# Merge of three attention patterns: one weight store and two weight loads per merge, products on GpSimd, z_b's product in the last stage

## Chip, cores and metric

One core of one Trainium2 chip. The metric is device time of one execution in microseconds (us), the median of the runs.

## What is computed

A hybrid encoder layer over 2048 tokens of width 1024, all in float32. The normalised input is projected to the inputs of a state-space branch, to queries, keys and values, to two gates z_a and z_b and to two mixing gates. The attention branch runs three dilated window patterns for 8 slots of 64 channels and merges them by their log-sum-exps:

```python
outs, lses = [], []
for p_idx, (window, dilation) in enumerate(ATTN_PATTERNS):
    o, lse = dilated_band_attention(q[:, :, p_idx], k, v, window, dilation)
    outs.append(o)
    lses.append(lse)
wts = jax.nn.softmax(jnp.stack(lses, axis=0), axis=0)
attn = jnp.einsum('gblh,gblhd->blhd', wts, jnp.stack(outs, axis=0)).reshape(bsz, L, ATTN_WIDTH)
y_b = (attn * jax.nn.silu(z_b)) @ w_proj_attn[layer].astype(jnp.float32)
...
mix = jax.nn.sigmoid(g_a) * y_a + jax.nn.sigmoid(g_b) * y_b
x = x + (mix @ w_out[layer].astype(jnp.float32)).astype(x.dtype)
```

## The kernel before, in words

Products on TensorE (PE) are made in three passes: each factor is split into a rounded high part and a low part (`hi`, `lo`; ScalarE copies, VectorE subtracts), and `mm3` adds hi*hi, hi*lo and lo*hi. Everything between stages goes through DRAM scratch tensors.

There are three stages. The first (to about 1085 us) makes the projections and the state-space branch. The second is attention, `phase_b`: 4 pairs of heads (`hp`), for each the patterns 1, 0 and 2, for each pattern 4 blocks of 512 tokens (`quad`). A step scores (`attn_scores`; VectorE's masked minimum in line 1003, ScalarE's exponential in line 1007), transposes the probabilities on PE and copies them out of PSUM, alternately on ScalarE and VectorE (`attn_turn`, lines 1030 and 1032), and multiplies by the values (`attn_values`). Between steps PE gets filler (`run`): gate projections, then the state-space branch's GLU, then the first parts of its output projection (`ssm_part`, weights `ws`). Queries (line 960) and values (lines 965, 972) are loaded by GpSimd's (POOL's) queue, almost all else by SyncE's (SP's).

When pattern 2 of a block of a pair is done, its merge starts: 16 merges, `attn_merge(hp, r, ...)`. A merge has three parts. The first transposes the block's minima and sums, stores them in ST and loads those of all three patterns (`s6`). The second works out the three weights per token on VectorE and ScalarE (lines 1096 to 1104), stores them in AL by two transfers (line 1108), one per head, and loads them back spread over the 64 channels of each head: six transfers of 128 KB (line 1111) into three tiles `ab[2]`, `ab[1]`, `ab[0]`, which share four buffers; then it loads z_b's block. The third multiplies and adds, five operations on POOL and one on VectorE, and stores the result in ACTB:

```python
G.tensor_mul(ab[2], ab[2], o2)
G.tensor_mul(ab[1], ab[1], self.O[1][:, c])
G.tensor_add(ab[2], ab[2], ab[1])
V.tensor_mul(ab[0], ab[0], self.O[0][:, c])
G.tensor_add(ab[2], ab[2], ab[0])
G.tensor_mul(ab[2], ab[2], zb)
```

The last stage, `phase_c`, goes over 8 blocks of 256 tokens. Two blocks need one merge of each of the four pairs. `cut` loads a block of ACTB and splits it (lines 1349, 1350, the tiles `pair`), PE projects it with `wa` (matmuls that read `wah` and `wal`), VectorE mixes it with the state-space part `cm` under the gates (lines 1401 to 1404, tiles `mh`, `ml`), PE multiplies by `wo`, and VectorE adds the input `xres`.

The source order is not the order of execution: the Tile framework's scheduler (`schedule_with_timeline_sim=True`, line 1495) lists each engine's instructions anew, with the source order as priority, and puts tiles of closed pools' memory to new use. Each engine and each queue then takes its list in order, so whoever waits holds all that is listed behind it.

## Time and profile before

| what | value |
|---|---|
| runs | 2077.11 us median of 3 (2076.78 to 2082.68) |
| profiled execution | 2084.98 us, span of its instructions 2083.2 us |
| busy share of the span | PE 95%, VectorE (DVE) 62%, ScalarE (ACT) 35%, POOL 40% |
| mean granted clock of TensorE | 0.974 |
| instructions | 37578 |

The profile is of one execution. Busy time is what an engine spent inside instructions; a waiting engine is idle, and "waits" name who ended the idle time. The windows cut the span into stretches: 1200 to 1680 is most of attention, with all but the last four of its merges (first merge's products at 1225.8 us), 1680 to 1760 its end with the last four merges and the start of the last stage, 1760 to 2083 the rest of the last stage. PEclk is the granted clock, 1.00 for 2.4 GHz. The chain of waits follows back from the last instruction.

### The profile page before, as it was taken

The page shows a single profiled execution, that of the slowest core. Times are in us where ns is not written, and L with a number is a line of the kernel's source. Part 1 is how long each engine was busy: PE and PEld are TensorE (multiplying, and loading weights), DVE is VectorE, ACT ScalarE, POOL GpSimd, SP SyncE. Part 2 cuts the span into 40 slices and gives each one's busy share as a digit, 9 for nine tenths or more (in the row PEclk, how much of TensorE's full clock was granted, in tenths as well). Part 3 has the DMA queues.
Part 4 walks back from the last instruction along what each step waited for, and adds up shares of the span by engine and source line. Part 5 has one row for each costly group of instructions (what it writes and reads, how often), then busy time and mean ns, then how long its engine had stood idle before and what let it go on. Part 6 is the DMA issues. An engine that isn't in the chain of part 4 may idle for free.

```text
span 2083.2 us, 37578 instructions
## 1 busy us (share of the span) xinstructions
PE 1975.6 (95%) x13612; PEld 1764.6 (85%) x13612; DVE 1292.2 (62%) x3312; ACT 725.7 (35%) x1829; POOL 826.8 (40%) x1088
## 2 busy tenths in 40 slices
PE   6899999999999999899989999998998978999999
PEld 6788899998788889899977877876887978899997
DVE  8867575978566778587755455455567655433432
ACT  4221343333232343233326544554655632100110
POOL 4310464538636654475442346346345222000000
PEclk9999999999999999999999999999998998999999
DMA  5632464445533444634474465566676547433332
GB/s 192 195 100 73 126 198 147 121 120 158 166 109 114 153 144 141 178 114 133 130 230 138 154 180 165 166 178 179 208 204 179 161 134 233 147 114 115 117 111 76
DMA packets 272059, 312.54 MB, mean 150 GB/s; under 512 B 86594, under 2 KB 182226, under 8 KB 271874
## 3 DMA queue, kind: packets, MB, share of 16 engines
q1 hardware_dynamic: 250914, 260.39, 41.8%
q0 software_dynamic: 20960, 49.76, 8.1%
q8 instruction: 107, 1.75, 0.3%
q14 instruction: 78, 0.64, 0.1%
HBM read 202.12 MB, written 105.71 MB: 148 GB/s over the span
## 4 chain that ended last, share of the span: by engine, by line
PE 59%; DVE 16%; DMA 13%; SPq 4%; issue 3%; POOL 3%; ACT 2%; DVEq 0%; ACTq 0%; POOLq 0%
PE acc L53 39%; PE po L53 12%; PE s L53 3%; PE pp L56 3%; DMA raw<-in_w_in 2%; DVE wlo L311 2%; DMA ab<-AL 2%; SPq L513 1%; DVE zs L843 1%; DMA AL<-e 1%; DMA ACTA<-fth 1%; DVE zs L841 1%; DMA s<-ST 1%; PE y L53 1%; SPq L1111 1%
## 5 line engine op out<-in xcount | busy, mean ns | idle before, releaser
L53 PE MATMUL acc<-xh,whi 128*128 128x512 f32 (+1 forms) x960 | 376.7, 393 | 17.8 <-DVE xsc L379 8.3
L53 PE MATMUL acc<-whi,xh 128*128 128x256 f32 x1280 | 368.2, 288 | 2.9 <-ACT qr L451 2.1
L53 PE MATMUL acc<-xl,whi 128*128 128x512 f32 (+1 forms) x960 | 367.9, 384 | 1.1 <-DVE xl L208 1.1
L53 PE MATMUL acc<-xh,wlo 128*128 128x512 f32 (+1 forms) x960 | 367.3, 384 | 0.0
L53 PE MATMUL acc<-whi,xl 128*128 128x256 f32 x1280 | 364.7, 285 | 1.9 <-POOL xl L263 1.6
L53 PE MATMUL acc<-wlo,xh 128*128 128x256 f32 x1280 | 364.7, 285 | 0.0
L53 PEld LDWEIGHTS acc<-whi,xh 128*128 128x128 f32 x1280 | 247.9, 194 | 5.6 <-ACT qr L451 2.4
L53 PEld LDWEIGHTS acc<-whi,xl 128*128 128x128 f32 x1280 | 247.9, 194 | 2.5 <-POOL xl L263 1.9
L53 PEld LDWEIGHTS acc<-wlo,xh 128*128 128x128 f32 x1280 | 248.1, 194 | 0.0
L53 PEld LDWEIGHTS acc<-xh,whi 128*128 128x128 f32 x960 | 184.9, 193 | 54.0 <-issue 10.9
L1007 ACT ACTIVATE p<-p,st 128x256 f32<-128x256 f32 (+2 forms) x384 | 172.8, 452 | 143.6 <-DVE st L1003 143.2
L311 DVE TENSOR_TENSOR wlo<-raw,whi 128x512 fp32r<-128x512 f32 x168 | 151.2, 918 | 110.9 <-ACT whi L310 110.1
L53 PEld LDWEIGHTS acc<-xh,wlo 128*128 128x128 f32 x960 | 184.9, 193 | 33.7 <-issue 0.5
L53 PEld LDWEIGHTS acc<-xl,whi 128*128 128x128 f32 x960 | 185.4, 193 | 29.4 <-DVE xl L208 1.6
L310 ACT ACTIVATE whi<-raw 128x512 fp32r<-128x512 f32 x176 | 102.9, 625 | 165.7 <-DMA raw<-in_w_in 140.1
L1003 DVE CUSTOM_DVE_ANT_0 p<-s,m 128x256 f32<-128x256 f32 (+2 forms) x376 | 115.8, 358 | 68.3 <-PE s L53 45.0
L972 POOL DMA_DIRECT2D v<-V x150 | 91.7, 618 | 121.2 <-PE po L53 115.0
L53 PE MATMUL s<-kh,q 128*128 128x256 f32 (+2 forms) x400 | 104.3, 299 | 12.1 <-DVE st L1003 7.2
L53 PE MATMUL acc<-pair,wsh 128*128 128x256 f32 x512 | 99.3, 295 | 16.3 <-DVE cm L1373 11.4
L53 PE MATMUL po<-t,v 128*64 128x128 f32 (+1 forms) x1280 | 110.3, 293 | 1.8 <-ACT t L1030 0.9
L56 PE MATMUL pp<-c_ident,p 128*128 128x128 f32 (+1 forms) x640 | 94.1, 281 | 13.5 <-DVE t L1032 12.4
L53 PEld LDWEIGHTS po<-t,v 128*64 128x64 f32 (+1 forms) x1280 | 75.3, 141 | 37.2 <-issue 23.7
(331 smaller groups left out, 4392.1 us busy)
## 6 DMA issues: line engine op xcount, KB each, us to landing
raw<-in_w_in SPq DMA_DIRECT2D x176, 256.0 KB
q<-QT POOLq DMA_DIRECT2D x92, 256.0 KB, 4.2
ab<-AL SPq DMA_DIRECT2D x96, 128.0 KB
ug<-U SPq DMA_DIRECT2D x128, 64.0 KB
GA<-th SPq DMA_DIRECT2D x32, 256.0 KB
GB<-th SPq DMA_DIRECT2D x32, 256.0 KB
raw<-GB SPq DMA_DIRECT2D x32, 256.0 KB
xres<-in_x SPq DMA_DIRECT2D x32, 256.0 KB
```

Of the source, the lines that this page charges most:

```text
L53: return self.nc.tensor.matmul(*a, **k)
L56: return self.nc.tensor.transpose(*a)
L310: self.nc.scalar.activation(hi, t, AF.Copy)
L311: (eng or self.nc.vector).tensor_sub(lo, t, f(hi))
L513: nc.sync.dma_start(at(dst, d, e), f(t[64 * h:64 * h + 64]))
L841: V.tensor_tensor_scan(zs[:64, n, 2:258], r[:64].to_broadcast([64, 256]), z[:64, n], 0.0, op0=OP.mult, op1=OP.add)
L843: V.tensor_tensor_scan(zs[64:, n, 0:256][:, ::-1], r[64:].to_broadcast([64, 256]), z[64:, n, ::-1], 0.0, op0=OP.mult, op1=OP.add)
L972: (nc.gpsimd if late else nc.sync).dma_start(v[:(16 if p == 0 else 4) * (j1 - j0), m - m0], at(self.V, (base + 4 * j0) * C + c0, rows + [[ ...
L1003: self.marks["dve"] = nc.vector.tensor_tensor_reduce(pt, sc, mk, op0=OP.add, op1=OP.min, scale=-0.125, scalar=least if o else 3e38, accum_ ...
L1007: self.marks["act"] = nc.scalar.activation(pt, pt, AF.Exp, bias=st[:, 0, h, c:c + 1], scale=-1.0, accum_out=st[:, 1, h, c:c + 1])
L1111: nc.sync.dma_start(t[64 * h:64 * h + 64], at(self.AL, hp * 6 * R + p * 2 * R + h * R + 512 * r, [[0, 64], [1, 512]]))
```

## The change

AL is laid out by pair, block, pattern, head and token, so that a merge's weights lie together. A merge stores them by one transfer and loads them by two, one per head with all three patterns, into one tile `ab` with two buffers of three patterns each. All its products are on POOL, and the one with z_b is gone from it. `cut` gets a further argument: in the last stage the block of z_b is loaded whole, and POOL multiplies it with the block of ACTB ahead of the split. The tiles `zb` and `xres` are in a pool of the last stage, no longer in attention's.

```diff
--- before.py
+++ after.py
@@ -109,7 +109,7 @@
         self.KT = scr("KT", [8, 2, 2, 64, 2048])
         self.V = scr("V", [2048, 512])
         self.ST = scr("ST", [4, 3, 2, 2, 2048])
-        self.AL = scr("AL", [4, 3, 2, 2048])
+        self.AL = scr("AL", [4, 4, 3, 2, 512])
         self.ACTA = scr("ACTA", [8, 128, 4, 256])
         self.ACTB = scr("ACTB", [4, 4, 128, 512])
 
@@ -1102,24 +1102,20 @@
             V.tensor_add(mn, mn, t[:, 2])
             V.reciprocal(mn, mn)
             V.tensor_mul(e, e, vw(mn, 0, [[0, 3], [1, 8]]))
-        ab = {p: mg.tile([128, 512], F32, name="ab", bufs=4) for p in (2, 1, 0)}
+        ab = mg.tile([128, 3, 512], F32, name="ab", bufs=2)
+        o = (4 * hp + r) * 3072
+        nc.sync.dma_start(at(self.AL, o, [[8, 128], [1024, 3], [1, 8]]), e)
         for h in range(2):
-            o = hp * 6 * R + h * R + 512 * r
-            nc.sync.dma_start(at(self.AL, o, [[8, 64], [2 * R, 3], [1, 8]]), e[64 * h:64 * h + 64])
-        for p, t in ab.items():
-            for h in range(2):
-                nc.sync.dma_start(t[64 * h:64 * h + 64], at(self.AL, hp * 6 * R + p * 2 * R + h * R + 512 * r, [[0, 64], [1, 512]]))
-        zb = self.op.tile([128, 512], F32, name="zb", tag="zb", bufs=2)
-        nc.sync.dma_start(zb, self.ZB[r, hp])
+            nc.sync.dma_start(ab[64 * h:64 * h + 64], at(self.AL, o + 512 * h, [[0, 64], [1024, 3], [1, 512]]))
         yield
         c = slice(512 * r, 512 * r + 512)
+        ab = [ab[:, p] for p in range(3)]
         with self.behind():
             G.tensor_mul(ab[2], ab[2], o2)
             G.tensor_mul(ab[1], ab[1], self.O[1][:, c])
             G.tensor_add(ab[2], ab[2], ab[1])
-            V.tensor_mul(ab[0], ab[0], self.O[0][:, c])
+            G.tensor_mul(ab[0], ab[0], self.O[0][:, c])
             G.tensor_add(ab[2], ab[2], ab[0])
-            G.tensor_mul(ab[2], ab[2], zb)
         nc.sync.dma_start(self.ACTB[r, hp], ab[2])
         yield
 
@@ -1340,14 +1336,18 @@
             for _ in self.ssm_part(b, self.early[b]):
                 yield 0.32 if _ is None else 0.0
 
-    def cut(self, src, scale):
+    def cut(self, src, scale, by=None):
         nc, V = self.nc, self.nc.vector
         hi, lo = self.pair()
         nc.sync.dma_start(f(lo), src)
+        x = f(lo)
+        if by is not None:
+            x = by
+            nc.gpsimd.tensor_mul(x, x, f(lo))
         for q in range(2):
             s = slice(2 * q, 2 * q + 2)
-            nc.scalar.activation(hi[:, s], f(lo[:, s]), AF.Copy, scale=scale)
-            V.scalar_tensor_tensor(lo[:, s], f(lo[:, s]), scale, f(hi[:, s]), op0=OP.mult, op1=OP.subtract)
+            nc.scalar.activation(hi[:, s], x[:, s], AF.Copy, scale=scale)
+            V.scalar_tensor_tensor(lo[:, s], x[:, s], scale, f(hi[:, s]), op0=OP.mult, op1=OP.subtract)
         return hi, lo
 
     def proj(self, b, w, y, g, gate):
@@ -1389,7 +1389,10 @@
             wcut = lambda: self.wcut(ws[0], None, 2)
             for b in range(8):
                 nb, o = b // 2, 256 * (b % 2)
-                bb = self.cut(at(self.ACTB, nb * 4 * 128 * 512 + o, [[512, 128], [128 * 512, 4], [1, 256]]), 0.5)
+                zb = cr.tile([128, 4, 256], F32, name="zb", bufs=2)
+                io = nb * 4 * 128 * 512 + o, [[512, 128], [128 * 512, 4], [1, 256]]
+                nc.sync.dma_start(zb, at(self.ZB, *io))
+                bb = self.cut(at(self.ACTB, *io), 0.5, zb)
                 mx = self.mixes.pop(b)
                 mh = self.op.tile([128, 8, 256], F32R, name="mh", tag="o0")
                 ml = self.op.tile([128, 8, 256], F32R, name="ml", tag="o1")
@@ -1412,7 +1415,7 @@
                     s = 4 * (2 * (b % 2) + t) + nb
                     for n in range(2):
                         rows = [[NS * D, 128], [1, 512]]
-                        xr = self.op.tile([128, 512], F32, name="xres", tag="zb", bufs=2)
+                        xr = cr.tile([128, 512], F32, name="xres", bufs=2)
                         nc.sync.dma_start(xr, at(self.ins["x"], s * D + 512 * n, rows))
                         ps = po.tile([128, 512], F32, name="po")
                         for k in range(8):
```

How the instructions stand in the built programs, at three places. In these rows x2 or x6 counts equal instructions in a row, numbers behind names tell buffers apart, and lines of the changed kernel are its own (products: L1114 to L1118, the weights' store L1107 and loads L1109, z_b's load L1394 and product L1346).

VectorE at the first merge, between the minima of scores and the copies of transposed probabilities, before:

```order
L1003 ISA p_14367,st<-s,m_12503 128x192
L1003 ISA st 128x1
L1120 TENSOR_TENSOR ab<-ab,o_12518 128x512
L1096 TENSOR_TENSOR mn<-s_14246 128x8
L393 TENSOR_SCALAR th<-th 128x512
L1097 TENSOR_TENSOR mn<-mn,s_14246 128x8
L1098 TENSOR_TENSOR e<-mn,s_14246 128x24
L311 TENSOR_TENSOR wlo<-raw,whi 128x512
L1032 COPY t_14392<-pp 128x384
```

and now:

```order
L1003 ISA p_14348,st<-s,m_12503 128x192
L1003 ISA st 128x1
L1096 TENSOR_TENSOR mn<-s_14237 128x8
L1097 TENSOR_TENSOR mn<-mn,s_14237 128x8
L1098 TENSOR_TENSOR e<-mn,s_14237 128x24
L393 TENSOR_SCALAR th<-th 128x512
L311 TENSOR_TENSOR wlo<-raw,whi 128x512
L1032 COPY t_14373<-pp 128x384
```

The product of line 1120, which reads a loaded `ab`, is gone from ahead of the copy `t`.

SP at the first merges, before:

```order
L1086 DMA ST<-sr_14243 4x4x128
L1108 DMA AL<-e 64x3x8 x2
L1089 DMA s_14246<-ST 64x6x8
L1111 DMA ab<-AL 64x512 x6
L1089 DMA s_14246<-ST 64x6x8
L1086 DMA ST<-sr_14358 4x4x128
L302 DMA raw<-in_w_in 128x512 x2
L1089 DMA s_14361<-ST 64x6x8 x2
L395 DMA GA<-th 128x512
L302 DMA raw<-in_w_in 128x512
L1108 DMA AL<-e 64x3x8 x2
L1111 DMA ab<-AL 64x512 x2
```

and now:

```order
L1086 DMA ST<-sr_14234 4x4x128
L1107 DMA AL<-e 128x3x8
L1089 DMA s_14237<-ST 64x6x8
L1109 DMA ab<-AL 64x3x512 x2
L1089 DMA s_14237<-ST 64x6x8
L302 DMA raw<-in_w_in 128x512 x2
L1086 DMA ST<-sr_14339 4x4x128
L1089 DMA s_14342<-ST 64x6x8 x2
L395 DMA GA<-th 128x512
L302 DMA raw<-in_w_in 128x512
L1107 DMA AL<-e 128x3x8
L1109 DMA ab<-AL 64x3x512 x2
```

Each merge has three issues where it had eight; what lies between them is nearly as it was.

SP at the end of attention, from the last merge's weights to the last stage, before:

```order
L1346 DMA pair<-ACTB 128x4x256
L1360 DMA raw<-GB 128x2x256
L1360 DMA cg<-GA 128x2x256
L1360 DMA raw<-GB 128x2x256 x2
L1360 DMA cg<-GA 128x2x256
L1123 DMA ACTB<-ab 128x512
L1108 DMA AL<-e 64x3x8 x2
L1416 DMA xres<-in_x 128x512
L1111 DMA ab<-AL 64x512 x6
L302 DMA raw<-in_w_out 128x512 x3
L1346 DMA pair<-ACTA 128x1024
L1360 DMA raw<-GB 128x2x256
L302 DMA raw<-in_w_out 128x512 x2
L1123 DMA ACTB<-ab 128x512
```

and now:

```order
L1107 DMA AL<-e 128x3x8
L1360 DMA raw<-GB 128x2x256
L302 DMA raw<-in_w_out 128x512
L1360 DMA cg<-GA 128x2x256
L1109 DMA ab<-AL 64x3x512 x2
L1342 DMA pair<-ACTA 128x1024
L1119 DMA ACTB<-ab 128x512
L302 DMA raw<-in_w_out 128x512
L1119 DMA ACTB<-ab 128x512
L1394 DMA zb<-ZB 128x4x256
L1419 DMA xres<-in_x 128x512 x2
L1394 DMA zb<-ZB 128x4x256
```

Before, the first block of ACTB (`pair<-ACTB`) is loaded ahead of the last merge's weights, and nothing else is needed for its split. Now z_b's first load stands behind the store of the last merge (the load of the block itself still stands ahead), and on POOL the block's product stands behind the last merge's five operations.

## Rows read from the trace of the kernel before

**Rows 1.** The page, part 1: busy time, share, instructions of each engine.

```profile
PE 1975.6 (95%) x13612; PEld 1764.6 (85%) x13612; DVE 1292.2 (62%) x3312; ACT 725.7 (35%) x1829; POOL 826.8 (40%) x1088
```

**Rows 2.** Windows: length, busy PE, PEld, DVE, ACT, POOL; PE clock, DMA share, GB/s.

```profile
1200.00:1440.00 240.00, 223.80 (x1520) 177.13 (x1518) 125.56 (x484) 113.91 (x402) 120.08 (x166) 0.96 0.61 173
...
1680.00:1760.00 80.00, 61.05 (x452) 57.75 (x451) 44.45 (x93) 20.20 (x49) 27.27 (x21) 0.87 0.63 178
1760.00:2083.00 323.00, 319.45 (x1984) 288.56 (x1983) 119.61 (x177) 38.11 (x64) 0.00 (x0) 1.00 0.39 120
```

**Rows 3.** Waits of PE, 1200 to 1440: total us, times, longest.

```profile
PE pp L56 <- DVE t L1032: 14.5, 6, 3.4
```

**Rows 4.** Waits of PE, 1440 to 1680.

```profile
PE pp L56 <- DVE t L1032: 4.0, 3, 2.0
```

**Rows 5.** Waits of DVE, 1200 to 1760.

```profile
DVE ab L1120 <- DMA ab<-AL: 44.0, 11, 6.2
```

**Rows 6.** Timeline of DVE: start, us, instruction, idle before it and releaser.

```profile
1230.20 1.68 DVE L1120 TENSOR_TENSOR ab<-ab,o 128x512 f32<-128x512 f32 x1 [4.84 <-DMA ab<-AL]
...
1423.83 2.50 DVE L1120 TENSOR_TENSOR ab<-ab,o 128x512 f32<-128x512 f32 x1 [5.19 <-DMA ab<-AL]
```

**Rows 7.** Timeline of PE, after those two.

```profile
1234.86 0.38 PE L56 MATMUL pp<-c_ident,st 128*16 128x128 f32 x1 [3.35 <-DVE t L1032]
...
1426.58 1.70 PE L56 MATMUL pp<-c_ident,p 128*64 128x128 f32 x7 [3.10 <-DVE t L1032]
```

**Rows 8.** A window behind the first of these gaps.

```profile
1232.00:1242.00 10.00, 7.14 (x32) 4.85 (x33) 6.92 (x30) 3.99 (x14) 1.46 (x2) 0.66 0.41 112
```

**Rows 9.** The tile ab: ns min/median/max, first and last start; its waits.

```profile
L1117 POOL TENSOR_TENSOR ab<-ab,o x16: 1267/1284/1377, 1225.8 to 1745.1; 128x512 f32<-128x512 f32 x16
...
L1120 DVE TENSOR_TENSOR ab<-ab,o x16: 679/1188/3230, 1230.2 to 1749.4; 128x512 f32<-128x512 f32 x16
...
  DMA ab<-AL: 116.2, 29
```

**Rows 10.** Timeline of SP, 1678 to 1756: issues of the last merges' transfers.

```profile
1678.18 0.63 SPq L1086 DMA_DIRECT2D ST<-sr  x1
...
1702.32 0.46 SPq L1123 DMA_DIRECT2D ACTB<-ab  x1
...
1729.58 0.38 SPq L1346 DMA_DIRECT2D pair<-ACTB  x1
...
1736.68 1.26 SPq L1108 DMA_DIRECT2D AL<-e  x2
...
1741.16 3.67 SPq L1111 DMA_DIRECT2D ab<-AL  x6
...
1755.62 0.38 SPq L1123 DMA_DIRECT2D ACTB<-ab  x1
```

**Rows 11.** Waits of PE, 1680 to 1760.

```profile
PE acc L53 <- DVE cm L1373: 11.4, 3, 5.1
PE acc L53 <- DVE mn L1096: 4.5, 1, 4.5
PE acc L53 <- DVE raw L1401: 2.6, 1, 2.6
```

**Rows 12.** Timeline of ACT and PE: the last stage's first block.

```profile
1736.40 1.15 ACT L1349 ACTIVATE pair<-pair 128x512 fp32r<-128x512 f32 x2 [0.82 <-DMA pair<-ACTB]
...
1739.37 0.40 PE L53 MATMUL acc<-pair,wah 128*128 128x256 f32 x2
```

**Rows 13.** Timeline of SP, and the chain of waits: a later block.

```profile
1801.21 0.36 SPq L1346 DMA_DIRECT2D pair<-ACTB  x1
...
1833.38 8.63 PE acc L53 x72
```

**Rows 14.** Timeline of DVE: line 1120 in the first and last of four merges.

```profile
1695.45 1.31 DVE L1120 TENSOR_TENSOR ab<-ab,o 128x512 f32<-128x512 f32 x1 [4.53 <-DMA ab<-AL]
...
1749.44 0.69 DVE L1120 TENSOR_TENSOR ab<-ab,o 128x512 f32<-128x512 f32 x1 [5.57 <-DMA ab<-AL]
```

## The prediction

> **What bounds the kernel now.** I read the engines' busy shares first, then stages in windows, then what TensorE (PE) waited for. PE is busy 95% of the span [rows 1], so an edit that adds no PE work can only win back time in which PE stands, or runs at the lower clock. The windows say where that is: in the attention stage PE stands 16.2 us of 240 between 1200 and 1440, in the change to the last stage 19.0 us of 80, in the last stage 3.6 us of 323; the granted clock goes with it, 0.96, 0.87 and 1.00 [rows 2]. So the merges can be worth some tens of microseconds and no more.
>
> Between 1200 and 1440 nearly all of PE's standing, 14.5 us in 6 times, is a transpose waiting for DVE's copies of transposed probabilities (line 1032) [rows 3]; from 1440 to 1680 that wait is 4.0 us [rows 4]. Why is DVE late? Its largest wait in the whole attention stage is line 1120, the merge's product with pattern 0, for the loads of the weights: 44.0 us, 11 times [rows 5]. DVE takes its instructions in order, so the copies stand behind that product. The first case: DVE stood 4.84 us and started line 1120 at 1230.20; PE, which had run out of copies, stood 3.35 us until 1234.86. The last of five such pairs in this window: DVE stood 5.19 us to 1423.83, PE 3.10 us to 1426.58 [rows 6, 7]. The five take 14.0 of the 14.5 us. Behind such a gap PE also comes back slower: the granted clock was 0.66 over the 10 us from 1232, a mix of its two levels, 1.2 and 2.4 GHz [rows 8].
>
> **The change, part by part.**
>
> *The DVE product goes to POOL.* DVE then waits for no weight loads. In 1200 to 1440 that gives back the five gaps, **14.0 us**, and the clock behind them: 0.04 of 240 us is 9.6 us if every drop there is of this cause [rows 2]; nothing if other gaps keep the clock down. I take **5**, half, since other short gaps stay. In 1440 to 1680 one of three gaps, the longest with 2.0 us, follows such a wait [rows 4]: **2.0**. DVE is also relieved of 16 products of 1.19 us (median) [rows 9], 19 us in all; it is busy 126 of 240 us there [rows 2], so I count that at nothing.
>
> *POOL.* Per merge it had five operations and keeps five: one product comes from DVE, the one with z_b leaves. Each lasts about 1.28 us [rows 9], so POOL's load is unchanged. What is queued behind POOL's wait are the issues of q and v loads. That wait can grow: POOL's first product needed two of six loads, now it needs both large ones. Below, nothing is gained; above, POOL's and DVE's waits of today, 116.2 us in 29 times [rows 9], all stand on POOL and some loads of q come late. I take zero, because the weights arrive together sooner (next item), and keep the loss as a rival.
>
> *SP's queue.* Per merge two stores and six loads took 1.26 and 3.67 us of issue [rows 10], and the z_b load, taken like the one-piece store of the same size, about 0.4: some 5.3 us. Now there are one store and two loads. The nearest rows are these same loads, 0.6 each; larger ones cannot be shown here, so 1.9 to 4.9 us. I take 1.9, as the time went per issue. That is 3.4 us per merge, 54 us of queue; it is worth something only where a chain through SP ends last, at the end of the attention.
>
> *The last four merges, and z_b.* Today the store of merge 13 is issued at 1702.32, that of merge 16 at 1755.62: 17.8 us apart each [rows 10]. Take off 3.4 of SP issue and 3.4 of DVE's wait per merge (it stood 4.53 us before the first and 5.57 before the last of these four products [rows 14]; I take less, since not all four wait), and the spacing is 11 us: the last store at about 1702 + 33 = 1735. That is sooner. But the built order puts the load of z_b for the first block of the last stage behind that last store on SP, and its product behind the last merge on POOL. Today the first block needs merge 13 alone: its load goes out at 1729.58, ScalarE cuts it at 1736.40 and PE takes up the block (wah) at 1739.37 [rows 10, 12]. Now, from 1735: 0.4 issue, 5 landing (6.8 for the row just named, with its queueing), 2.6 product (twice the 512-wide 1.28) and 1.2 cut, so about 1744: **5 us later** than today, and a spell of the lower clock behind the stand, **+3.4** (6.8 us at half rate, as the 0.66 over 10 us amounts to). One later wait of today, 2.6 us for DVE's mixing of that block [rows 11], falls in the shadow: **-2.6**. PE's earlier stands in this window, 4.5 and 11.4 us [rows 11], don't count separately: they only decide how long PE waits at the block. Behind that split, on ScalarE and DVE, stand the splits of w_out's pieces, which the first output product needs; they are next to be late, but PE has 96 matmuls of the block (11 us, at the 8.63 us for 72 of [rows 13]) to cover them. Net **+6**. Bounds: a merge alone takes 24.1 us from its first store to its last (1678.18 to 1702.32), which would put the last store at 1726 and the block at 1735, -7 in all; with the last store where it is today, the block starts near 1765, +26.
>
> *The other seven blocks.* Their loads go out some 32 us before use (1801.21, used at 1833.38) [rows 13]. One more load in parallel and a 2.6 us product fit under that. Nothing counted; if the cover went, 8 times 2.6, 21 us, would be the price.
>
> Against this item speaks one row: line 1120 lasts 0.68 us at best and 3.23 at worst [rows 9], that is, DVE's two-input operations get slower when POOL works beside them. The Trainium skill, page "SBUF — State Buffer", section "Who interferes with whom", says why it may: a DVE instruction with two SBUF inputs and a GpSimd one that reads SBUF share a read port, and whichever starts second is blocked until the first is through. By that rule the eight new products could each hold a DVE instruction for their whole length, and the sum would lose up to 21 us instead of nothing; the trace agrees that such stretching happens, not that PE feels it.
>
> **Sum.** -14.0 -5 -2 +6 = -15 us. The profiled execution took 2084.98 us (span 2083.2), 7.9 above the median; the same -15 from the median 2077.11 gives **2062 us**.
>
> **Rivals.**
> - *The new wait decides (slower).* The last store does not move forward, since the last four merges still go through SP one behind another. Then z_b, loaded behind it, starts the block near 1765: +26; the gaps are won (14 and 2), the clock is not: 2077 + 26 - 16 = 2087. For it: SP also carries the gate and weight loads, in which it stands for DVE. Against it: DVE's 4 to 5 us stands are gone from the chain. Even with the clock won (21 us in all) gain turns into loss once the last store comes after about 1750 of today's time. Chance 0.16.
> - *The wait moves to POOL.* Its products stand for weights, q and v loads come late, and PE waits for scores where it now waits for copies: the 14, 5 and 2 are lost, the tail is as forecast: 2077 + 6 = 2083. For it: POOL already stands in 18 of those 29 waits. Against it: PE's 16.2 us of standing from 1200 to 1440 hold 14.5 for the copies [rows 2, 3], so a late q costs nearly nothing today. Chance 0.14.
> - *The tail shortens as well.* A last store at 1726 and the whole clock: -14 -9.6 -2 -7, so 2045. Chance 0.13.
> - *The read port holds DVE in the last stage.* Each of eight products stops a DVE operation for all of its 2.6 us and PE waits for it: 2062 + 21 = 2083. Against it: DVE is busy 120 of 323 us there [rows 2], and the output products have four accumulators to run ahead in. Chance 0.05.
> - *It does not do what it says*: the order written anew puts other waits on DVE and nothing remains but noise, 2077. Chance 0.04.
>
> **How the numbers follow.** The forecast itself has 0.48. A measurement of this kernel tells about 0.3%, 6.2 us, from no change. Faster by more: 0.44 of the forecast's 0.48, 0.13 of the short tail and 0.04 of the POOL case, which may be partial: 0.61. Slower by more: 0.13 of the new wait, 0.03 each of POOL and port: 0.19. The rest, 0.20, is within. For 8 in 10 the range runs from 2048, short of the best case, to 2086, short of the worst.
>
> **What would show it.** Right: no DVE wait for ab left; PE's waits for line 1032 from 1200 to 1440 down from 14.5 to under 3 us; clock near 1 there; the load of z_b issued after the last store, and one long stand of PE (10 to 20 us) before the first wah. Wrong: PE waiting for q or scores behind POOL; a stand above 30 us before wah, which would mean that the last merges did not get faster; or gaps in the last stage.

## The result and the profile after

The changed kernel takes 2092.8 us, the kernel before 2077.0: **ratio 1.0068, 95% interval 1.0050 to 1.0086, slower by 0.7%.** The forecast was 2062 us, range 2048 to 2086; the time lies outside it and on the other side of no change.

The profiled execution took 2090.18 us, its span is 2088.2. That is only 5.2 us more than the profiled execution of the kernel before (2084.98), though the medians differ by 15.8. That execution of before was a long one, as a second profile of it shows below, and this one is the shortest of the changed kernel's four.

The page of the changed kernel, part 1 (beside [rows 1]):

```profile
PE 1968.8 (94%) x13612; PEld 1761.1 (84%) x13612; DVE 1288.5 (62%) x3296; ACT 726.0 (35%) x1829; POOL 849.1 (41%) x1096
```

Its windows (beside [rows 2]; columns as there):

```profile
1200.00:1440.00 240.00, 226.84 (x1546) 180.73 (x1545) 120.56 (x475) 113.56 (x396) 124.61 (x168) 0.97 0.60 168
1440.00:1680.00 240.00, 224.04 (x1882) 202.65 (x1881) 162.24 (x547) 144.00 (x460) 95.14 (x133) 0.96 0.60 174
1680.00:1760.00 80.00, 47.53 (x339) 45.78 (x339) 40.13 (x70) 18.22 (x34) 29.45 (x21) 0.79 0.68 198
1760.00:2088.00 328.00, 324.45 (x2018) 293.55 (x2016) 120.65 (x176) 35.63 (x59) 16.93 (x7) 1.00 0.40 123
```

The last stage runs as before. In 1680 to 1760 PE now stands 32.5 us where it stood 19.0, and the clock is 0.79 where it was 0.87. In 1200 to 1440 it still stands 13.2 us, and the clock is 0.97. The waits of PE in that window (beside [rows 3]):

```profile
PE pp L56 <- DVE t L1032: 6.9, 3, 3.1
PE pp L56 <- DVE sr L1085: 5.6, 4, 3.2
```

The first was to fall from 14.5 to under 3 us. The second, for the copies of the transposed statistics (line 1085), was 1.1 us in the kernel before.

The waits of DVE, 1200 to 1760 (us in total, times, longest), where [rows 5] had 44.0 us for ab:

```profile
DVE p L1003 <- PE s L53: 49.7, 33, 4.2
DVE mn L1096 <- DMA s<-ST: 35.9, 8, 6.6
```

No wait for ab is left, as forecast. But line 1096, the merge's first minimum, waits 35.9 us for the loads of its statistics. In the kernel before, the same view has 16.4 us for it. In DVE's list it stands in front of the same copies as line 1120 did. One case, timeline of DVE and then of PE:

```profile
1244.13 0.27 DVE L1096 TENSOR_TENSOR mn<-s 128x8 f32<-128x8 f32 x1 [4.95 <-DMA s<-ST]
...
1249.70 0.54 DVE L1032 COPY t<-pp 128x384 f32<-128x384 f32 x1
```

```profile
1250.30 0.66 PE L56 MATMUL pp<-c_ident,p 128*128 128x128 f32 x4 [2.95 <-DVE t L1032]
```

DVE stood 4.95 us for the statistics, its copies came late, and PE stood 2.95 us for them: the picture of [rows 6, 7] with another load in it.

The longest stand of PE for a copy, later in attention, has no load behind it. Timelines of DVE and PE, and the durations of line 1153 (ns: least, median, most):

```profile
1580.64 5.50 DVE L1153 SCALAR_TENSOR_TENSOR pair<-ft,pair 128x512 fp32r<-128x512 f32 x1
```

```profile
1586.66 0.69 PE L56 MATMUL pp<-c_ident,p 128*128 128x128 f32 x2 [5.69 <-DVE t L1032]
```

```profile
L1153 DVE SCALAR_TENSOR_TENSOR pair<-ft,pair x16: 671/691/5501, 1449.1 to 1658.6; 128x512 fp32r<-128x512 f32 x16
```

This DVE operation lasted 5.50 us while POOL made merge products beside it (from 1581.19); in the second profile of this kernel (after_again, below) the longest of line 1153 is 2.12 us.

The end of attention. The tile view gives the number of an instruction, its durations, and its first and last start. First the last products of attention (they read t), then those with wah, for the kernel before:

```profile
L53 PE MATMUL po<-t,v x1280: 269/273/476, 1095.6 to 1693.0; 128*64 128x128 f32 x161, 64*64 64x128 f32 x22
...
L53 PE MATMUL acc<-pair,wah x512: 277/283/387, 1739.4 to 2058.4; 128*128 128x256 f32 x171
```

and for the changed kernel:

```profile
L53 PE MATMUL po<-t,v x1280: 269/273/476, 1093.5 to 1684.9; 128*64 128x128 f32 x161, 64*64 64x128 f32 x22
...
L53 PE MATMUL acc<-pair,wah x512: 277/283/582, 1744.9 to 2063.4; 128*128 128x256 f32 x171
```

From the last attention product to the first wah it was 46.4 us and is 60.0. I call this stretch the tail. Timelines of SP, POOL, ACT and PE in it:

```profile
1696.52 0.38 SPq L1119 DMA_DIRECT2D ACTB<-ab  x1
...
1714.43 0.36 SPq L1107 DMA_DIRECT2D AL<-e  x1
...
1721.97 1.24 SPq L1109 DMA_DIRECT2D ab<-AL  x2
...
1735.69 0.32 SPq L1119 DMA_DIRECT2D ACTB<-ab  x1
1737.93 0.37 SPq L1394 DMA_DIRECT2D zb<-ZB  x1
```

```profile
1741.84 2.34 POOL L1346 TENSOR_TENSOR zb<-zb,pair 128x1024 f32<-128x1024 f32 x1 [6.17 <-DMA zb<-ZB]
```

```profile
1744.21 1.15 ACT L1349 ACTIVATE pair<-zb 128x512 fp32r<-128x512 f32 x2 [4.37 <-POOL zb L1346]
```

```profile
1744.90 1.31 PE L53 MATMUL acc<-pair,wah 128*128 128x256 f32 x3 [20.58 <-ACT pair L1349]
```

The chain is the forecast's: last store, z_b's load, its product, the split, wah; PE stands 20.58 us in one piece. What holds z_b's load back stands in the queue's own waits, 1735 to 1742:

```profile
SPq L1394 <- DMA ACTB<-ab: 1.5, 1, 1.5
```

It waits for the last merge's store to be done, though it reads nothing of it. The likely reason is that the tile lies in memory of attention's closed pools; the experiments on theory 1 bear on it.

### The profile page after: what moved, and what is told of

The parts are those of the page before. It is cut to its first block, busy times and chain, and to the rows that moved or that the text cites. A ratio compares the mean times of both kernels' runs of the same rounds, so it can differ in the third digit from the quotient of the medians.

```text
span 2088.2 us, 37441 instructions
## 1 busy us (share of the span) xinstructions
PE 1968.8 (94%) x13612; PEld 1761.1 (84%) x13612; DVE 1288.5 (62%) x3296; ACT 726.0 (35%) x1829; POOL 849.1 (41%) x1096
## 4 chain that ended last, share of the span: by engine, by line
PE 61%; DVE 15%; DMA 11%; SPq 4%; issue 4%; POOL 3%; ACT 2%; DVEq 0%; ACTq 0%; POOLq 0%
PE acc L53 41%; PE po L53 12%; PE s L53 3%; PE pp L56 3%; DMA ST<-sr 2%; DMA raw<-in_w_in 2%; DVE wlo L311 2%; SPq L513 1%; DMA s<-ST 1%; PE y L53 1%; DVE zs L843 1%; PE tp L56 1%; DMA mr<-kk 1%; DMA AL<-e 1%; DVE zs L841 1%
## 5 line engine op out<-in xcount | busy, mean ns | idle before, releaser
L53 PEld LDWEIGHTS acc<-xh,wlo 128*128 128x128 f32 x960 | 184.8, 193 | 33.8 <-issue 0.4
L1346 POOL TENSOR_TENSOR zb<-zb,pair 128x1024 f32<-128x1024 f32 x8 | 19.3, 2408 | 249.8 <-DMA pair<-ACTB 233.5
L53 PE MATMUL acc<-pair,wah 128*128 128x256 f32 x512 | 95.6, 288 | 21.0 <-ACT pair L1349 20.6
```

Source lines behind the costliest of these rows:

```text
L53: return self.nc.tensor.matmul(*a, **k)
L1346: nc.gpsimd.tensor_mul(x, x, f(lo))
```

## Experiments

Theory 1: the tail costs, because z_b's load and product come behind the last merges. Theory 2: attention does not gain, because DVE's wait for the statistics takes the place of its wait for ab. Theory 5, formed after the first runs: the new layout costs by itself, through the size of its loads (5a) or its two whole buffers (5b). Rivals: the loss is in POOL's longer chain (3), PE's gaps in attention have another cause (4), or the scheduler's order differs from build to build (5d).

In the table, "tail" is the time from the start of the last attention product to the first wah. The waits are for 1200 to 1690: DVE for ab and for the statistics (s), and SP, at the issue of their loads, the store of the statistics. Ratios are to the kernel before, measured beside each kernel.

| kernel | ratio, 95% interval | last attention product | tail | DVE for ab | DVE for s | SP for ST |
|---|---|---|---|---|---|---|
| before, first profile | | 1693.0 | 46.4 | 30.6 | 16.4 | 16.7 |
| copy (of before) | 1.0008 [0.9996, 1.0020] | 1682.0 | 45.3 | 33.7 | 16.6 | 19.2 |
| changed | 1.0068 [1.0050, 1.0086] | 1684.9 | 60.0 | 0 | 35.9 | 34.9 |
| after_again (changed) | 1.0069 [1.0046, 1.0092] | 1679.1 | 61.4 | 0 | 35.8 | 34.3 |
| zb_only | 1.0048 [1.0033, 1.0063] | 1678.5 | 67.4 | 39.4 | 18.8 | 20.4 |
| zb_mem | 1.0068 [1.0048, 1.0089] | 1681.9 | 58.4 | 0 | 34.3 | 33.1 |
| split | 0.9986 [0.9969, 1.0002] | 1686.4 | 41.4 | 0 | 36.3 | 34.5 |
| pool_only | 0.9967 [0.9953, 0.9981] | 1682.0 | 44.1 | 0 | 27.9 | 18.0 |
| dve_back | 1.0133 [1.0109, 1.0157] | 1704.7 | 63.9 | 33.8 | 16.1 | 31.8 |
| stat_const | 0.9962 [0.9944, 0.9980] | 1662.6 | 59.1 | 0 | 0 | 37.5 |
| early_after | 1.0063 [1.0047, 1.0078] | 1682.9 | 62.7 | 0 | 46.2 | 40.0 |
| early_stat | 0.9956 [0.9942, 0.9971] | 1672.3 | 46.6 | 0 | 41.4 | 25.8 |
| old_al | 0.9937 [0.9921, 0.9953] | 1672.7 | 49.2 | 0 | 24.0 | 20.7 |
| six_loads | 0.9956 [0.9942, 0.9970] | 1678.2 | 41.7 | 0 | 27.6 | 20.5 |
| singles6 | 0.9937 [0.9917, 0.9956] | 1680.1 | 39.3 | 0 | 25.1 | 18.4 |
| one_store | 0.9888 [0.9867, 0.9910] | 1668.6 | 44.0 | 0 | 22.0 | 20.8 |
| pool_one_store | 0.9944 [0.9929, 0.9960] | 1686.4 | 41.4 | 0 | 21.4 | 22.3 |

Ratios are from several executions, the other columns from one profile each, so they need not follow each other to the microsecond. Some profiled executions lie far from their kernel's median: dve_back 11.9 us above it, one_store 6.8, pool_one_store 6.2 and zb_only 5.3 above, after_again 6.3 below.

### Second profiles of the two kernels

Unchanged copies.

> The kernel before, unchanged, for a second profile. Every theory: within 0.2% of the kernel before (2077 us), ratio 1.000. The first profiled execution of the kernel before took 2084.98 us, 8 above its median; if that was chance in one execution, this profile's execution lies near 2077 and the stages in which it is shorter show where the 8 us were; if profiling itself costs 8 us, it lies near 2085 again.

> The changed kernel, unchanged, for a second profile. Every theory: ratio 1.007 to the kernel before, some 2092 us. Stages, if the first profile was a usual execution: attention ends at 1683 to 1688, PE stands 28 to 31 us from the first score's values to the end of attention, and again 15 to 21 us in one piece before the first wah.

The twelve executions of the copy took 2072.8 to 2082.1 us, so the first profile, with 2084.98, was at the long end. This one's execution took 2075.18. The copy's window and PE's wait there, beside [rows 2, 3]:

```profile
1200.00:1440.00 240.00, 231.65 (x1577) 184.06 (x1576) 127.36 (x496) 118.02 (x414) 125.97 (x173) 0.97 0.63 178
```

```profile
PE pp L56 <- DVE t L1032: 5.4, 6, 2.7
```

Its last attention products and its products with wah:

```profile
L53 PE MATMUL po<-t,v x1280: 269/273/476, 1095.7 to 1682.0; 128*64 128x128 f32 x161, 64*64 64x128 f32 x22
...
L53 PE MATMUL acc<-pair,wah x512: 277/283/416, 1727.3 to 2048.6; 128*128 128x256 f32 x171
```

Attention ends 11 us earlier than in the first profile. PE stands 8.4 us in the window, not 16.2, and waits 5.4 us for the copies, not 14.5. DVE's wait for ab, 1200 to 1760, is nearly as long as in [rows 5]:

```profile
DVE ab L1120 <- DMA ab<-AL: 41.9, 11, 5.7
```

In 1200 to 1440 alone it is 23.0 us, against 28.0 in the first profile. So DVE waits of nearly the same size cost PE 14.5 us in one execution and 5.4 in another, and the forecast's largest term was read from the costlier one. The changed kernel's two profiles agree in what matters: tail 60.0 and 61.4, DVE's wait for s 35.9 and 35.8. Against the expectation, attention ends at 1679.1 in the second, earlier than 1683, and PE's stand before the first wah is 23.8 us, longer than 21:

```profile
L53 PE MATMUL po<-t,v x1280: 269/273/476, 1090.5 to 1679.1; 128*64 128x128 f32 x161, 64*64 64x128 f32 x22
```

From its first product with t to its last, attention took 597.4 and 586.3 us in the two profiles of the kernel before, 591.4 and 588.6 in those of the changed one. Whatever the change gained there is less than the difference between two executions of one kernel.

### Theory 1: the tail

z_b's move alone, made in the kernel before (the edits of `cut`, `zb` and `xres` from the change; z_b's load and product leave the merge):

> The kernel before with z_b's product moved to the last stage and nothing else. Theory 1 (the tail: z_b's load and product behind the last merge make PE stand before the last stage's first block): the merges keep their old pace, so the last store stays near 1755 and the first wah comes near 1765 instead of 1739; less some waits that fall in its shadow, 15 to 22 us slower, 2092 to 2099 us. Rival (the loss of the change comes from the merge's loads or from the product on GpSimd): at most 4 us slower, up to 2081.

Slower by 0.48%, 10 us: less than the 15 to 22 expected, but the sign and the place are theory 1's. PE's waits, 1660 to 1765:

```profile
PE acc L53 <- ACT pair L1350: 20.9, 1, 20.9
```

The tail is 67.4 us against 45.3 in the copy, 22 us more. Attention is 3 us shorter (first to last product 583.4 against 586.3), with one operation and one load less in each merge, and this execution was 5.3 us above the kernel's median, so the 22 is at the large end.

In zb_mem the place of z_b's tile is changed:

```diff
+        self.mg = ap("mg", ctx=base, side="right")
...
-        self.mg = ap("mg", **R)
...
-                zb = cr.tile([128, 4, 256], F32, name="zb", bufs=2)
+                zb = self.mg.tile([128, 4, 256], F32, name="zb", tag="ab", bufs=2)
...
-                        xr = cr.tile([128, 512], F32, name="xres", bufs=2)
+                        xr = self.ev.tile([128, 512], F32, name="xres", tag="e1")
```

> The changed kernel with the pool of the merges kept open in the last stage, z_b's tile in the two buffers of ab and xres in a tile of an older pool, so that z_b's first load waits for merge 15 instead of 16 and w_out's splits for no merge. Theory 1: z_b's product on GpSimd starts right after the last merge's (1735.7 instead of 1741.8) and the first wah comes 6 to 8 us earlier: 2085 to 2087 us. Rival (the last stage's first block waits for something else): within 2 us of the changed kernel's 2093.

No gain in time by the ratio (1.0068 both); the 6 to 8 us expected did not come. The load went out earlier, at 1730.20, but the product still stood behind the last merge's five on POOL, from 1735.59 to 1738.4, and the tail is 58.4. Freeing the load alone was not enough.

In split z_b's tiles have a pool of their own, opened first; w_out's tiles are in two pools, and xres in a tile of an older pool:

```diff
+            cz = self.pool("cz", ctx=ctx, side="right")
             cr = self.pool("cwr", ctx=ctx, side="right")
+            cr = cr, self.pool("cwr1", ctx=ctx, side="right")
...
-            wo = [[cr.tile([128, 8, 512], F32R, name=f"wo{n}{c}") for n in "hl"] for c in range(2)]
+            wo = [[cr[c].tile([128, 8, 512], F32R, name=f"wo{n}{c}") for n in "hl"] for c in range(2)]
...
-                zb = cr.tile([128, 4, 256], F32, name="zb", bufs=2)
+                zb = cz.tile([128, 4, 256], F32, name="zb", bufs=2)
...
-                        xr = cr.tile([128, 512], F32, name="xres", bufs=2)
+                        xr = self.ev.tile([128, 512], F32, name="xres", tag="e1")
```

> The changed kernel with z_b's two tiles in a pool of their own in the last stage, opened first, so that they lie over attention's keys alone, and w_out's tiles in two pools; xres in a tile of an older pool. In the built order z_b's first load then stands ahead of the last four merges' loads, and the block's product between merges 14 and 15. Theory 1 (the place of z_b's tile in memory makes its load, and with it the product, come behind the last merges): the stand before the first wah, 16 to 21 us so far, goes nearly to 0, and 15 to 20 us are won against the changed kernel: 2073 to 2078 us. Rival (the last merges hold the tail up in another way, PE then stands at the next block or at w_out): at most 5 us won, 2088 to 2093.

2075.6 us, 0.82 percentage points below the changed kernel: 17 us, as theory 1 expected. Timelines of SP and POOL:

```profile
1672.17 0.38 SPq L1396 DMA_DIRECT2D zb<-ZB  x1
```

```profile
1714.08 1.62 POOL L1118 TENSOR_TENSOR ab<-ab 128x512 f32<-128x512 f32 x1
1715.66 2.41 POOL L1346 TENSOR_TENSOR zb<-zb,pair 128x1024 f32<-128x1024 f32 x1
1721.74 1.26 POOL L1114 TENSOR_TENSOR ab<-ab,o 128x512 f32<-128x512 f32 x1 [3.66 <-DMA ab<-AL]
```

The load is issued before attention ends and the product stands between merges 14 and 15. The tail is 41.4 us and PE's wait for the split of the block is gone. So in the changed kernel z_b was late through the memory its tile was given, which the last merges still held, and through its place on POOL. The product itself costs little: the tail is no longer than the copy's 45.3 us.

### The product on GpSimd

Alone in the kernel before (`V.tensor_mul(ab[0], ...)` becomes `G.tensor_mul`), and taken back alone in the changed kernel:

> The kernel before with the product of line 1120 moved from VectorE to GpSimd and nothing else. Theory 2 (VectorE's wait for ab is replaced by its wait for the merge's statistics, line 1096): DVE's wait for ab goes from 44 us to 0, its wait for s rises from 16 to some 30 us, and the time stays within 8 us of the kernel before, 2069 to 2079. The forecast's own mechanism: 14 to 21 us faster, 2056 to 2063. Rival 3 (GpSimd's longer chain makes q and v late): 4 to 12 us slower.

> The changed kernel with the product with pattern 0 back on VectorE; z_b's move and the new layout of AL stay. Theory 2: DVE waits for ab again and less for s; within 6 us of the changed kernel, 2087 to 2099 us. If the product on GpSimd alone is worth what it was in the kernel before (-6.8 us): 2098 to 2100. Rival 3 (five products in a row on GpSimd are what costs in the change): 4 to 10 us faster, 2083 to 2089.

pool_only is 0.33% faster, 7 us, inside theory 2's range (at most 8 us faster) and short of the forecast's 14 to 21. Its waits of DVE (1200 to 1690) have none for ab, and 27.9 us where the copy has 16.6:

```profile
DVE mn L1096 <- DMA s<-ST: 27.9, 7, 6.4
```

Its profile does not show where the 7 us are. Attention is no shorter than the copy's (590.3 us against 586.3, first to last product); its first product comes 4 us earlier:

```profile
L53 PE MATMUL po<-t,v x1280: 269/273/477, 1091.7 to 1682.0; 128*64 128x128 f32 x161, 64*64 64x128 f32 x22
```

dve_back is slower than the changed kernel by 0.65 percentage points, some 13 us. In its profile PE's wait (1200 to 1690) is twice the changed kernel's 15.4 us, but that execution took 2113.89 us, 11.9 above the median:

```profile
PE pp L56 <- DVE t L1032: 30.4, 10, 7.7
```

Rival 3 falls by the times: this part of the change gains in both pairs. Of how the gain comes about only the vanished wait for ab is shown.

### Theory 2: the wait for the statistics

In stat_const the weights are worked out from a constant tile; the statistics are still stored and loaded, but no operation reads them:

```diff
+        self.sk = []
...
+        if not self.sk:
+            self.sk.append(mg.tile([128, 3, 2, 8], F32, name="sk"))
+            V.memset(self.sk[0], 1.0)
...
         yield
+        s6 = self.sk[0]
         mn = mg.tile([128, 8], F32, name="mn")
```

> The changed kernel with the weights worked out from a constant tile instead of the loaded statistics (store and loads of the statistics are still issued, so that the queues carry the same; the weights are then all one third). DVE waits neither for ab nor for s. Theory 2 (the wait for s, 35.9 us on DVE, took the place of the wait for ab and kept the gaps in PE): PE's waits for line 1032 from 1200 to 1690 fall from 15 us to under 5, attention ends 10 to 20 us earlier, 2073 to 2083 us. Rival 4 (these gaps have another cause, such as DVE's own work or the filler's order): within 4 us of the changed kernel, 2089 to 2097.

22 us faster than the changed kernel (0.9962 against 1.0068), attention ends at 1662.6 instead of 1684.9, and the tail is as long as it was. PE's wait for the copies, 1200 to 1690, is 5.8 us where the changed kernel has 15.4 (expected: under 5). The window and the attention products:

```profile
1200.00:1440.00 240.00, 238.98 (x1681) 192.48 (x1681) 128.44 (x512) 126.73 (x433) 131.00 (x178) 1.00 0.65 180
```

```profile
L53 PE MATMUL po<-t,v x1280: 269/273/476, 1092.2 to 1662.6; 128*64 128x128 f32 x161, 64*64 64x128 f32 x22
```

PE stands 1.0 us of 240 and the clock is 1.00. That is what the forecast promised of this window; of the kernels run, only this one, in which DVE waits for neither load, has it. So the wait for the statistics did hold PE there. How much of the 22 us it is stays less sure, since stat_const is also another build, in which a merge's later steps need not wait for the statistics either, and builds differ by some 10 us (below). one_store, in which DVE still waits 22.0 us for s, gets through attention in 569.9 us, as fast as stat_const with 570.4:

```profile
L53 PE MATMUL po<-t,v x1280: 269/273/474, 1098.7 to 1668.6; 128*64 128x128 f32 x161, 64*64 64x128 f32 x22
```

A real way to it was tried twice, on the changed kernel and on old_al: the merge's first part one step earlier.

```diff
-            self.merges.append(self.attn_merge(hp, quad, x["st"], g["o2"]))
+            m = self.attn_merge(hp, quad, x["st"], g["o2"])
+            next(m)
+            self.merges.append(m)
...
+        yield
         yield
```

> The same edit on the changed kernel (2093 us), with its large loads and its late z_b. Theory 2: DVE's wait for the statistics falls from 35.9 us to under 10, 8 to 20 us faster, 2073 to 2085. Rival 4: within 4 us, 2089 to 2097.

> The kernel old_al with the merge's first part (the transpose, store and loads of the statistics) run in the same step in which the block's values are done, one step earlier than before, and a free step before the weights are worked out. Theory 2 (VectorE's wait for the statistics, 24 us there, is what still makes PE stand in attention): the wait falls to under 8 us, attention ends 4 to 10 us earlier, 2055 to 2061 us. Rival 4 (the gaps have other causes, or the earlier transposes make PE wait for the minima): 2063 to 2068.

Both missed. By the ratios early_stat is 4 us slower than old_al, early_after 1 us faster than the changed kernel. DVE's wait did not fall, it rose; in early_stat, where old_al has 24.0 us:

```profile
DVE mn L1099 <- DMA s<-ST: 41.4, 12, 6.5
```

In the executed order the first minimum had moved up too: in 11 of the 16 merges fewer DVE instructions lie between it and the copy of its statistics than in old_al, in the second merge 15 where there were 24. The wait was not taken away, so this doesn't test theory 2, and how to take it away in earnest stays open. With 17 us more of DVE's wait the time rose by 4 us, and PE waited 6.3 us for line 1032 (old_al 7.7) and 9.4 for the copies of statistics (5.7): again a DVE wait has no fixed price in PE's gaps.

### Theory 5: the new layout and its two large loads

old_al is split with the old AL: two stores, six loads of 128 KB, four single buffers. six_loads is split with these lines:

```diff
-        for h in range(2):
-            nc.sync.dma_start(ab[64 * h:64 * h + 64], at(self.AL, o + 512 * h, [[0, 64], [1024, 3], [1, 512]]))
+        for p in (2, 1, 0):
+            for h in range(2):
+                nc.sync.dma_start(ab[64 * h:64 * h + 64, p], at(self.AL, o + 1024 * p + 512 * h, [[0, 64], [1, 512]]))
```

> The kernel split, with the weights' old layout of AL: two stores and six loads per merge into four single buffers. Everything else as split. If the new layout is worth nothing: within 3 us of split. If its fewer issues help SP at the last merges (3.4 us each): 4 to 10 us slower than split. Rival (two large loads into two buffers hold the merges up): 4 to 10 us faster than split.

> The kernel split with six loads of 128 KB per merge, one per head and pattern, instead of two of 384 KB; one store, the new AL, and the two buffers of three patterns stay. Split took 2075.6 us, old_al 2064.6. Theory 5a (the two large loads are what the new layout costs: the merge's statistics, which are stored and loaded behind them, come late): 2064 to 2068 us, and SP's wait for the store of the statistics falls from 34.5 us to about 20. Theory 5b (two buffers of three patterns, freed only when a merge's result is stored, are what it costs): 2073 to 2078, SP's wait for the store of ab before line 1109 stays at about 15 us.

old_al is 0.49 percentage points, 10 us, faster than split, so the new layout as a whole costs in this order. Six loads instead of two win 0.30 percentage points of it, 6 us. The queue's own waits (SP, 1200 to 1690), of split and then of six_loads:

```profile
SPq L1089 <- DMA ST<-sr: 34.5, 11, 6.1
```

```profile
SPq L1089 <- DMA ST<-sr: 20.5, 11, 4.1
```

The wait fell to "about 20", as theory 5a expected. SP's wait for the store of ab before these loads, the sign of theory 5b, stayed (14.8 and 14.3 us), so it is not what the 6 us came from. The wait for ST divides the whole table: 31.8 to 40.0 us in the seven profiles with two loads of 384 KB per merge, 16.7 to 25.8 in the ten with six of 128 KB. The statistics' store is 8 KB in the view of the DMA issues.

SP has less to issue with two loads and so comes sooner to the wait; that alone would lengthen it. But the store itself is done later. The third merge's, in split and in six_loads, with the issue that waits for it (timelines of SP):

```profile
1216.85 0.65 SPq L1086 DMA_DIRECT2D ST<-sr  x1
1223.60 0.58 SPq L1089 DMA_DIRECT2D s<-ST  x1
```

```profile
1220.33 0.65 SPq L1086 DMA_DIRECT2D ST<-sr  x1
...
1222.47 1.28 SPq L1089 DMA_DIRECT2D s<-ST  x2
```

It took 6.8 us from issue to the loads that wait for it in split and 2.1 in six_loads. By the semaphore signals in the traces, the stores of line 1086 (1087 or 1088 in some kernels) between 1190 and 1690 took 3.6 to 4.4 us on average from issue to their last signal in the seven profiles and 2.8 to 3.2 in the ten. The loads that DVE waits for can only start then. That the store's packets stand behind the loads' is the likely reason; no run shows it by itself.

The rest of the 10 us is less clear. one_store is old_al with the new AL and one store, six loads into four single buffers; singles6 has six such buffers; pool_one_store is pool_only with that store.

> The kernel old_al with the new AL and its one store per merge; the six loads into four single buffers stay. Theory 5a and theory 5b both: as old_al, 2062 to 2067 us. Rival 5c (the one store over 128 partitions, or reading from the new place, is slower than two): 2070 to 2076.

> The kernel one_store with six single buffers for ab instead of four: as much memory as the two buffers of three patterns of six_loads, but each freed by itself. Six_loads took 2067.9 us, one_store 2052.9. Theory 5b (buffers freed only as a whole, when the result is stored, hold the next merge's loads): 2050 to 2056 us. Rival 5d (the order that the scheduler finds differs by some 10 us from build to build, and the 15 us between these two are that): anything between 2050 and 2070, and a value above 2060 speaks for it.

> The kernel pool_only (the kernel before with the product with pattern 0 on GpSimd, z_b still multiplied in the merge) with the new AL and its one store, six loads into four single buffers. Pool_only took 2071.7 us. If one store instead of two is worth what it was between old_al and one_store: 2059 to 2063 us. Rival 5d (those 11.7 us were the order's luck): 2068 to 2075.

one_store is the fastest kernel of all, 2052.9 us, 1.1% below the kernel before; neither theory had said so. But singles6, which only adds two buffers to it, loses 0.49 points again, and its 2065.7 us lie above the 2060 that were to speak for rival 5d: builds that differ in nothing that was expected to cost differ by some 10 us. What in them does it, the order or the place of tiles in memory, was not looked into. The one store won 0.49 points on old_al and 0.23 on pool_only. Its sign is the same both times, though the second is hardly clear of noise; its size and theory 5b are left open. And rival 5d bears on every single pair of kernels here: a difference of 6 to 10 us between two builds, such as that of six_loads, is no proof by itself. The tail, the product on POOL and the large loads rest on two pairs each or on a wait that changed with them.

## Why the prediction was wrong

- **The five gaps, -14.0, and the clock, -5; the gap in 1440 to 1680, -2.** This is the step that failed: "DVE then waits for no weight loads. In 1200 to 1440 that gives back the five gaps". The first sentence held, the second didn't follow. DVE met the next load in its list, the statistics: its wait there went from 16.4 to 35.9 us, and PE stood 13.2 and 15.8 us (after_again) in a window where it had stood 16.2 or 8.4 before. In 1440 to 1680 PE's wait for line 1032 was 8.6 and 5.1 us in the two profiles where [rows 4] has 4.0; the longest stand of the first lies behind the slow operation of line 1153, not behind a load. The first half of the mechanism was right: DVE's stands do hold PE, and stat_const, with neither wait, won 22 us. That this is near the forecast's 21 is partly luck, by the next point and the spread of builds. The terms never asked what DVE waits for next, though the tail's did; the chance of 0.04 for other waits on DVE was all there was of it, and [rows 11] already had PE standing 4.5 us behind line 1096.
- **The size of the gaps.** Even with a good replacement the median had less to give than the profile: the terms came from an execution 7.9 us above the median, in which PE stood some 8 us more in just this window than in the copy. The prediction took the difference off the total and not off the terms.
- **SP's queue, 0.** One store and two loads took 0.36 and 1.24 us of issue in the last merge, 1.6 against the estimate of 1.9. The miss is what large loads do to small transfers around them: SP's wait for the store of the statistics rose from 16.7 and 19.2 us (two profiles) to 34.9, and six loads win 6 us back. The Trainium skill, page "DMA: Bandwidth & Descriptors", section "Rules for kernel authors", advises to coalesce many small transfers into one large one, and says that under 64 KB one pays mostly overhead. The six were 128 KB each, above that mark, and coalescing them did not pay here: six were 0.30 points faster than two (six_loads against split).
- **The last four merges, and z_b, +6.** Right in mechanism: last store, z_b's load, product, split, wah, and one stand of PE of 20.6 us (10 to 20). That the clock times fit too, last store at 1735.7 (forecast 1735) and wah at 1744.9 (1744), is luck: they were counted from merge 13's store at 1702 as in the kernel before, while by the prediction's own sum attention was to end 21 us earlier and all of this with it. Measured from the end of attention, the tail grew by 13.6 us in the profiles and 14.7 against the copy; without the late z_b (split) the kernel gains 17 us. The mis-sized part is mostly the spacing of the four stores, 11 us forecast: (1735.7 - 1696.5)/3 = 13.1, some 6 us over the three. Merge 13's store also came 11.6 us after the last attention product instead of 9.3.
- **The other seven blocks, 0, and the read port.** Right. The tile view has, for the eight products,

```profile
L1346 POOL TENSOR_TENSOR zb<-zb,pair x8: 2341/2418/2426, 1741.8 to 2002.3; 128x1024 f32<-128x1024 f32 x8
```

2.4 us each (2.6 forecast), and from the first wah to the end of the span it is 343.3 us, before 343.8 and in the copy 346.1. The eight products cost PE nothing in this stage; no run here shows any of the 21 us that were their possible price. The rule of the Trainium skill, page "SBUF — State Buffer", section "Who interferes with whom", that a DVE instruction with two SBUF inputs contends with a GpSimd one that reads SBUF, may stand behind another place: the 5.50 us of line 1153 in attention, beside POOL's merge products, behind which PE stood 5.69 us in one of the two profiles.
- **POOL, 0.** Right. POOL stood 52.1 and 60.9 us for the weights in the two profiles (1200 to 1690), 36.4 in the kernel before and 50.2 in the copy, but PE waited for neither q nor v there, and in both pairs the kernel with the product on POOL is the faster one.
- **The sum.** One part at a time, from the ratios: the product on POOL -7 us (pool_only), z_b's move +10 (zb_only), the layout with its large loads +10 (split against old_al): +13; the ratio of the changed kernel makes +14. So close a fit is partly luck, since each part is one pair of builds. By other pairs the last part is 6 us (six_loads) or 20 (split against one_store).
- **The rivals.** "The new wait decides" (2087) had the right side and the right place, but let the gaps be won. "It does not do what it says: the order puts other waits on DVE" had attention right, with a chance of 0.04 and a price of nothing. The time is the two together, which no case joined.

## What to carry to other kernels

When a wait is removed from an engine that works in order, look in the same list of waits for that engine's next load and see when it arrives: if it comes no earlier, the stall moves there and the gain is only the difference. Before a term is read from one profile, compare that execution with the median; if it is longer, the excess may lie in the very gaps that are to be won. And where a change moves an operation into a later stage, ask which memory its tile gets there and who holds it until when: here the same move made 17 us of difference, by the pool its tile was put in.

## What was not expected of the hardware

- Two loads of 384 KB instead of six of 128 KB moved the same bytes with less issue time, and 8 KB stores near them took longer, 3.6 to 4.4 us on average instead of 2.8 to 3.2; SP's total wait for them was 16.7 to 25.8 us with small loads and 31.8 to 40.0 with large ones.
- With DVE's merge waits gone (stat_const) the granted clock was 1.00 over the 240 us from 1200 in which it was 0.96 and 0.97 in the kernel before and 0.97 in the changed one; PE stood 1.0 us there instead of 16.2, 8.4 and 13.2.
- A DVE operation of line 1153, 0.67 us at best, lasted 5.50 us beside POOL's merge products in one execution and at most 2.12 in another.
- Executions of one built kernel differ by 0.4% (2072.8 to 2082.1 us for the copy), and between the two profiled ones of the kernel before, 9.8 us apart, attention accounts for all of it (last product at 1693.0 and 1682.0).
